# Rounding the attention weights on ScalarE and giving each of the first four attention steps three half projections

## The chip, the core and the metric

The kernel runs on one core of a Trainium2 chip. The time is that of the device for one launch, in microseconds (us): the median of three runs. One further run was taken with the hardware profiler; every row shown comes from that one.

## What is computed

One layer of a decoder: a mixer sublayer, a cross-attention to 256 memory tokens, and a SwiGLU feed-forward network, on 512 tokens of width 1024, in fp32. The change touches only the mixer, and in it only the causal stick-breaking attention (8 heads of 64) and the projections that run beside it:

```python
h = rms_norm(x, norm_mix[l])
proj = h @ w_in[l]
q_a, k_a, v_a, u_b, gate_b, gate_c, g_a, g_b = jnp.split(proj, split_points, axis=-1)
...
z = jnp.einsum('bhqd,bhkd->bhqk', qb, kb) * scale
log_fail = jnp.where(mask, jax.nn.log_sigmoid(-z), 0.0)
log_later = lax.cumsum(log_fail, axis=3, reverse=True) - log_fail
weights = jnp.where(mask, jnp.exp(jax.nn.log_sigmoid(z) + log_later), 0.0)
outs.append(jnp.einsum('bhqk,bhkd->bhqd', weights, vb))
```

## The kernel before

**Numbers in two parts.** TensorE is fed fp32r operands. To keep fp32 accuracy, every operand is split into a high part (the value rounded to fp32r, a copy) and a low part (value minus high part, a subtraction on VectorE), and each product is three matmuls: high by high, high by low, low by high (`mm3`, L154). For weights from memory the copy is on ScalarE (L150) and the subtraction on VectorE (L151).

**A projection** is one column block of 128 outputs: one load of 512 KB (L143, on SyncE's queue), the split, and 8 times three matmuls of 512 columns into one bank of `pmm`, a PSUM pool of two banks. It is done in two halves of 12 matmuls: `open_project` (L270) loads, splits and does the first half; `project` (L276) finishes it, and the caller (`qk_part`, `conv`, `gate`) reads the bank and frees it. Between the two halves the bank stays taken.

**An attention step** is one pair of heads `p` (0 to 3) with one block of 128 keys `kt`, taken from 3 down to 0; steps are numbered 0 to 15 in that order. It covers 128, 256, 384 or 512 queries of each of the two heads. For `kt` of 3 and 2 both heads share one tile of 256 or 512 columns, for 1 and 0 each has its own of 384 or 512.
- `scores` (L373): z on TensorE (L382 or L389); then `e` = softplus(z): Abs, Exp, Ln on ScalarE (L396 to L398), an add on VectorE (L399), the causal mask on GpSimd (`causal`, L355).
- `parts` (L408): adds the carry of the later key blocks (L420) and splits `e`: high part on ScalarE (L369), low part on VectorE (L370).
- `weights` (L428): TensorE adds the reverse cumulative sum into z's bank (L433, high part and then low part of each tile); the next carry (L438); `a` = Exp on ScalarE (L441); the mask on GpSimd (L355); then the high part `ah` (L449) and the low part `al` (L450), both on VectorE.
- `values` (L454): TensorE multiplies `ah` and `al` with the values (L461); after `kt` 0 the pair's output is copied, added and split (L469 to L472).

**The order of the work.** Within the loop over the steps (L519) TensorE's order is the program's: in step i it does its share of half projections, then `scores` of step i+1, `weights` of step i, `values` of step i-1. On the other engines a scheduler orders by its own estimate of when each instruction can start; `scores` and `parts` are raised in priority (100), the Exp of `weights` more so (150), the copies at L449 not. `fill_some` (L509) takes halves from a list of 22 column blocks, 44 halves in all: the next pair's q and k, then gate C, u and gate B of the convolution, pair after pair, and last four merge gates. After step i this many are done:

```python
FILL = ((3, 2, 3, 3), (2, 2, 3, 4))            # L33: first pair; each of the other three
shares = FILL[0] + (TT - 1) * FILL[1]          # L507
fill_some(n_fill * sum(shares[:i + 1]) / sum(shares))      # L524, rounded up by the loop of L510
```

At step 14 two small means are also taken through the same two banks of `pmm`: `var` at once after the share (L526), `varb` at the step's end (L538); `varb` is read by ScalarE (L121) and VectorE (L124). After the loop comes the merge, with sigmoids on ScalarE (L567) and one more gate.

Of the kernel before, what the change touches and what calls it, by code (L numbers as in the profile page):

```python
# [29 lines left out]
MEM_AT = (5, 7, 9, 11)  # L30
MEAN_AT = 14
EARLY = 2
FILL = ((3, 2, 3, 3), (2, 2, 3, 4))  # L33
WARM = 8
FIRST = 4

# [4 lines left out]
def hybrid_layer(ctx: ExitStack, tc: tile.TileContext, xT_d, memT_d, cols_d, wv_d, win_d,  # L41
                 wbr_d, wmix_d, wmq_d, wmk_d, wmv_d, wmo_d, wfi_d, wfo_d, out):
    nc = tc.nc
# [19 lines left out]
    def unit(s, cols=512):  # L63
        return upool.tile([P, cols], F32R, tag="u", name=nm(s), padded_shape=[P, 512])

    def tmp(s, cols=512):
        return tpool.tile([P, cols], F32, tag="t", name=nm(s), padded_shape=[P, 512])

    def f(ap):
        return ap.bitcast(F32)  # L70
# [273 lines left out]
    def span(kt):  # L344
        return kt * P, S - kt * P

    def by_head(t, kt):

        n = span(kt)[1]
        if 2 * n <= 512:  # L350
            return [t[0].rearrange("p (h n) -> p h n", n=n)]
        return [u[:, None, :] for u in t]

    def causal(t):
        nc.gpsimd.affine_select(out=t[:, :, :P], in_=t[:, :, :P], compare_op=ALU.is_gt, fill=0.0,  # L355
                                base=0, pattern=[[0, t.shape[1]], [1, P]], channel_multiplier=-1)
# [71 lines left out]
    def weights(p, kt):  # L428
        c0, n = span(kt)
        av[p, kt] = []  # L430
        for z, both in zip(zs[p, kt], sp[p, kt]):
            for part in both:
                nc.tensor.matmul(z, negtri, part, start=False, stop=True, skip_group_check=True)  # L433
        exp_a = []
        got = first.get((p, kt), [])
        with tc.high_priority(150):
            for r, z in zip(got, zs[p, kt]):
                nc.vector.tensor_tensor(out=r, in0=r, in1=z[0:1, :], op=ALU.subtract)  # L438
            for h, z in enumerate(zs[p, kt]):
                exp_a.append(tmp("a")[:, :z.shape[1]])  # L440
                exps.append(nc.scalar.activation(exp_a[h], z, AF.Exp))  # L441
            for h, r in enumerate(got):
                w = r.shape[1]
                nc.sync.dma_start(carries[kt % 2][P - 1:P, h * w:(h + 1) * w], r)
        for a in exp_a:
            causal(by_head([a], kt)[0])
            w = a.shape[1]
            ah, al = unit("ah")[:, :w], unit("al")[:, :w]
            nc.vector.tensor_copy(ah, a)  # L449
            nc.vector.tensor_tensor(out=al, in0=a, in1=f(ah), op=ALU.subtract)  # L450
            for i in range(w // n):
                av[p, kt].append((ah[:, i * n:(i + 1) * n], al[:, i * n:(i + 1) * n]))
# [53 lines left out]
    n_fill = len(fill)  # L506
    shares = FILL[0] + (TT - 1) * FILL[1]  # L507

# [9 lines left out]
    with tc.manual_schedule(engines={mybir.EngineType.PE}):  # L518
        for i in range(len(steps) + 1):  # L519
            if i in MEM_AT:  # L520
                mem_square(MEM_AT.index(i))
            if i == MEAN_AT - 2:
                mean = squares_mean(accm[:, 0, :], MT)
            fill_some(n_fill * sum(shares[:i + 1]) / sum(shares))  # L524
            if i == MEAN_AT:
                rm = mean[0]("rm", bank=mmtile)  # L526
            if i + 1 < len(steps):
                scores(*steps[i + 1])
            if i < len(steps):
                weights(*steps[i])  # L530
            else:
                gate(EARLY, 0)
            if i + 1 < len(steps):
                parts(*steps[i + 1])
            if i > 0:
                values(*steps[i - 1])
            if i == MEAN_AT:
                rmb = mean[1]("rmb", bank=mmtile)  # L538
# [555 lines left out]
```

## Time and profile before

| what | value |
|---|---|
| median of 3 runs | 860.76 us (860.56 to 861.03) |
| the profiled execution's own time | 860.98 us |
| its span, first to last instruction | 859.2 us |
| mean granted clock of TensorE | 0.999 |
| busy: PE, DVE, ACT, POOL | 850.5, 586.5, 431.1, 62.0 us |

In the rows, PE is TensorE's matmuls, PEld its weight loads, DVE is VectorE, ACT ScalarE, POOL GpSimd, SP SyncE. L12 is line 12 of the kernel. Matmuls are pipelined: a matmul of 512 columns shows as some 390 ns but the next starts after some 227 ns, so the distance of starts says how fast TensorE goes, and the busy column doesn't. A row of the timeline gives the start, the length of the merged rows, the engine, the line, the operation, output <- inputs, the count and, in brackets, the idle time before with what ended it.

### The profile page before, as it was taken

How to read it: one execution, taken by the hardware profiler on the slowest of the kernel's cores; microseconds unless marked ns; L12 is line 12 of the kernel's file. 1: busy time of each engine (PE TensorE's matmuls, PEld its weight loads, DVE VectorE, ACT ScalarE, POOL GpSimd, SP SyncE). 2: the span in 40 equal slices, each digit the busy share in tenths (PEclk: the TensorE clock that was granted, in tenths of full speed). 3: DMA queues.
4: the chain of work that ended last, by engine and by line, in shares of the span. 5: the costliest groups of instructions: out<-in, count | busy, mean ns of one | idle time of the engine just before them, and what ended most of it. 6: DMA issues, size and time to landing. Idle time of an engine off the chain costs nothing.

```text
span 859.2 us, 12693 instructions
## 1 busy us (share of the span) xinstructions
PE 850.5 (99%) x4912; PEld 748.6 (87%) x4912; DVE 586.5 (68%) x963; ACT 431.1 (50%) x750; POOL 62.0 (7%) x92
## 2 busy tenths in 40 slices
PE   9999999999999999999999999999999999999997
PEld 7877788888888898888888889999999999888897
DVE  8769898986454475555555779888887778533334
ACT  7566766665333344433444666555445556422335
POOL 1011111111000000000000101111111100000002
PEclk9999999999999999999999999999999999999999
DMA  8322331228333255422110527776777753322202
GB/s 295 132 90 77 120 111 62 74 99 266 111 103 111 96 177 184 143 98 98 50 67 33 137 54 202 187 182 172 185 188 195 182 147 127 119 98 99 73 1 98
DMA packets 42859, 108.34 MB, mean 126 GB/s; under 512 B 4656, under 2 KB 8752, under 8 KB 42800
## 3 DMA queue, kind: packets, MB, share of 16 engines
q1 hardware_dynamic: 36528, 95.72, 32.8%
q0 software_dynamic: 5984, 11.54, 8.2%
q8 instruction: 38, 0.62, 0.3%
q10 hardware_dynamic: 288, 0.29, 0.1%
q14 instruction: 21, 0.17, 0.1%
HBM read 104.36 MB, written 2.10 MB: 124 GB/s over the span
## 4 chain that ended last, share of the span: by engine, by line
PE 96%; DVE 2%; DMA 1%; issue 0%; POOL 0%; SPq 0%; DVEq 0%; ACT 0%; POOLq 0%
PE z L801 15%; PE y L801 7%; PE pr L155 7%; PE pr L156 7%; PE pr L157 7%; PE f L156 5%; PE f L157 5%; PE f L155 5%; PE v L801 4%; PE r L156 3%; PE r L155 3%; PE r L157 3%; PE v L261 3%; PE mq L156 2%; PE mq L157 2%; PE mq L155 2%
## 5 line engine op out<-in xcount | busy, mean ns | idle before, releaser
L150 ACT CAST wh<-wr 128x1024 fp32r<-128x1024 f32 x106 | 111.1, 1050 | 222.2 <-issue 98.6
L151 DVE TENSOR_TENSOR wl<-wr,wh 128x1024 fp32r<-128x1024 f32 x106 | 129.4, 1223 | 99.4 <-ACT wh L150 99.2
L155 PE MATMUL pr<-xgh,wh 128*128 128x512 f32 x288 | 112.6, 391 | 0.0
L156 PE MATMUL pr<-xgl,wh 128*128 128x512 f32 x288 | 112.4, 390 | 0.0
L157 PE MATMUL pr<-xgh,wl 128*128 128x512 f32 x288 | 112.3, 390 | 0.0
L156 PE MATMUL f<-actl,wh 128*128 128x512 f32 (+1 forms) x208 | 74.3, 357 | 0.0
L155 PE MATMUL f<-acth,wh 128*128 128x512 f32 (+1 forms) x208 | 74.2, 357 | 0.0
L157 PE MATMUL f<-acth,wl 128*128 128x512 f32 (+1 forms) x208 | 74.1, 357 | 0.0
L801 PE MATMUL z<-xdh,wf 128*128 128x256 f32 x352 | 70.4, 283 | 0.0
L157 PEld LDWEIGHTS pr<-xgh,wl 128*128 128x128 f32 x288 | 54.1, 188 | 11.3
L155 PEld LDWEIGHTS pr<-xgh,wh 128*128 128x128 f32 x288 | 54.1, 188 | 10.9
L156 PEld LDWEIGHTS pr<-xgl,wh 128*128 128x128 f32 x288 | 54.1, 188 | 10.8
L758 POOL DMA_DIRECT2D ws<-in_w_ffn_in_dram x22 | 26.6, 1208 | 469.0 <-DVE c L616 267.8
L801 PEld LDWEIGHTS z<-xdh,wf 128*128 128x128 f32 x352 | 58.0, 192 | 0.0
L821 ACT COPY sa<-z 128x256 f32<-128x256 f32 x44 | 16.4, 372 | 78.3 <-PE z L801 78.2
L801 PE MATMUL z<-xdl,wf 128*128 128x256 f32 x176 | 49.9, 283 | 0.0
L792 DVE TENSOR_TENSOR wf<-s,wf 128x512 fp32r<-128x512 f32 x44 | 30.3, 691 | 21.1 <-ACT wf L791 20.0
L155 PEld LDWEIGHTS f<-acth,wh 128*128 128x128 f32 x208 | 39.3, 189 | 5.8
L156 PEld LDWEIGHTS f<-actl,wh 128*128 128x128 f32 x208 | 39.3, 189 | 5.6
L157 PEld LDWEIGHTS f<-acth,wl 128*128 128x128 f32 x208 | 39.3, 189 | 5.5
L801 PE MATMUL v<-xoh,wf 128*128 128x256 f32 x176 | 35.5, 283 | 0.0
L801 PE MATMUL y<-xch,wf 128*128 128x256 f32 x176 | 35.5, 283 | 0.0
(281 smaller groups left out, 2134.8 us busy)
## 6 DMA issues: line engine op xcount, KB each, us to landing
wr<-in_w_in_dram SPq DMA_DIRECT2D x36, 512.0 KB, 3.3
ws<-in_w_ffn_in_dram SPq DMA_DIRECT2D x22, 512.0 KB, 3.8
wg<-in_w_ffn_in_dram SPq DMA_DIRECT2D x22, 512.0 KB, 4.2
ws<-in_w_ffn_in_dram POOLq DMA_DIRECT2D x22, 512.0 KB, 5.8
wr<-in_w_ffn_out_dram SPq DMA_DIRECT2D x22, 512.0 KB, 3.3
a<-in_w_ffn_in_dram SPq DMA_DIRECT2D x22, 256.0 KB, 4.5
wr<-in_w_branch_dram SPq DMA_DIRECT2D x8, 512.0 KB, 3.2
wr<-in_w_mem_k_dram SPq DMA_DIRECT2D x8, 512.0 KB, 3.2
```

Source lines behind the costliest of these rows:

```text
L150: after(nc.scalar.copy(h2, raw), lead[-1:])
L151: lows.append(nc.vector.tensor_tensor(out=l2, in0=raw, in1=f(h2), op=ALU.subtract))
L155: nc.tensor.matmul(ps, a[0], b[0], start=start, stop=False, **kw)
L156: nc.tensor.matmul(ps, a[0], b[1], start=False, stop=False, **kw)
L157: nc.tensor.matmul(ps, a[1], b[0], start=False, stop=stop, **kw)
L261: nc.tensor.matmul(vps[t], xg[k][a][:, sl], wv[k][b], start=k == 0 and (a, b) == (0, 0), stop=k == KD - 1 and a == 1)
L758: nc.gpsimd.dma_start(s13, a[:, 0:4:3, :], accum_op=ALU.add)
L792: nc.vector.tensor_tensor(out=lo, in0=raw, in1=f(hi), op=ALU.subtract)
L801: nc.tensor.matmul(ps[:, :HS], a, b, start=i < 3 and k == 0 and j == 0, stop=k == KP - 1 and j == 2, skip_group_check=True)
L821: nc.scalar.copy((s[:, :HS], None, None, s[:, HS:], t[:, :HS])[i], z)
```

## The change

Two edits. The copy that makes `ah` goes from VectorE to ScalarE, for all 24 tiles of attention weights. The shares of the first pair go from 3, 2, 3, 3 to 3, 3, 3, 3. The list still has 44 halves while the shares now add up to 45, and the loop rounds up, so the halves by step are

| step | 0 | 1 | 2 | 3 | 4 | 5 | 6 | 7 | 8 | 9 | 10 | 11 | 12 | 13 | 14 | 15 |
|---|---|---|---|---|---|---|---|---|---|---|---|---|---|---|---|---|
| before | 3 | 2 | 3 | 3 | 2 | 2 | 3 | 4 | 2 | 2 | 3 | 4 | 2 | 2 | 3 | 4 |
| after | 3 | 3 | 3 | 3 | 2 | 2 | 3 | 4 | 2 | 2 | 3 | 4 | 2 | 2 | 3 | 3 |

Step 1 gains one half and step 15 loses one; from step 1 to step 14 the list is one half further on, so that where a column block was finished and the next one opened, one is now opened and finished, and the other way round.

```diff
-FILL = ((3, 2, 3, 3), (2, 2, 3, 4))
+FILL = ((3, 3, 3, 3), (2, 2, 3, 4))
...
             ah, al = unit("ah")[:, :w], unit("al")[:, :w]
-            nc.vector.tensor_copy(ah, a)
+            nc.scalar.copy(ah, a)
             nc.vector.tensor_tensor(out=al, in0=a, in1=f(ah), op=ALU.subtract)
```

## Prediction

> **What bounds the kernel now.** I read the page's first part and its chain first, then the list of what TensorE waited for, then the attention stage by windows (the first pair of heads, and the last), then TensorE's timeline in that stage.
>
> ```profile
> span 859.2 us, 12693 instructions
> ...
> PE 850.5 (99%) x4912; PEld 748.6 (87%) x4912; DVE 586.5 (68%) x963; ACT 431.1 (50%) x750; POOL 62.0 (7%) x92
> ...
> PE 96%; DVE 2%; DMA 1%; issue 0%; POOL 0%; SPq 0%; DVEq 0%; ACT 0%; POOLq 0%
> ```
>
> ```profile
> PE z L433 <- DVE l L370: 0.9, 2, 0.5
> ```
>
> ```profile
> 28.70:77.00 48.30, 47.79 (x220) 38.43 (x221) 36.74 (x65) 28.94 (x57) 6.01 (x11) 1.00 0.28 94
> ...
> 155.00:193.00 38.00, 38.00 (x182) 31.23 (x181) 34.42 (x65) 24.34 (x48) 5.76 (x12) 1.00 0.24 84
> ```
>
> The chain is TensorE for 96% of the span. In the attention stage (20 to 210 us) TensorE is listed as waiting for one thing only: the low part `l` of step 1 and of step 3, 0.9 us in two waits. The windows (span, then busy PE, PEld, DVE, ACT, POOL) show why it is `l`: in the last pair's window VectorE is busy 34.42 of 38.00 us (91%), ScalarE 24.34 (64%). So no edit in this stage can win more than the time in which TensorE stands still, and the matmuls themselves are the same in number before and after. The timeline prices this, by starts:
>
> ```profile
> 49.54 0.39 PE L155 MATMUL pr<-xgh,wh 128*128 128x512 f32 x1
> ...
> 54.76 0.39 PE L157 MATMUL pr<-xgh,wl 128*128 128x512 f32 x1
> ...
> 55.79 0.49 PE L433 MATMUL z<-l,negtri 128*128 128x512 f32 x1
> 56.72 0.50 PE L433 MATMUL z<-l,negtri 128*128 128x512 f32 x1 [0.43 <-DVE l L370]
> 57.05 0.22 PE L461 MATMUL o<-ah,v 128*128 128x128 f32 x1
> ...
> 76.50 1.02 PE L433 MATMUL z<-l,negtri 128*128 128x512 f32 x3
> 77.99 0.50 PE L433 MATMUL z<-l,negtri 128*128 128x512 f32 x1 [0.47 <-DVE l L370]
> 78.33 0.33 PE L461 MATMUL o<-ah,v 128*128 128x384 f32 x1
> ```
>
> ```profile
> 92.64 0.73 PE L433 MATMUL z<-l,negtri 128*128 128x512 f32 x2
> 93.20 0.22 PE L461 MATMUL o<-ah,v 128*128 128x128 f32 x1
> ```
>
> ```profile
> 115.37 1.09 PE L433 MATMUL z<-l,negtri 128*128 128x512 f32 x4
> 116.30 0.33 PE L461 MATMUL o<-ah,v 128*128 128x384 f32 x1
> ```
>
> From the first two rows: 24 matmuls, so 23 distances in 5.22 us, 0.227 us each; **a half projection of 12 takes 2.72 us**. Step 1's `weights` took 57.05 - 55.79 = 1.26 us; the same step of the second pair, which didn't wait, 93.20 - 92.64 = 0.56: lost 0.70. Step 3's took 78.33 - 76.50 = 1.83 against 116.30 - 115.37 = 0.93: lost 0.90. **Together 1.60 us, 0.19% of the time, is all that the stage has to give by this reading.**
>
> **The change part by part.** *The third half in step 1.* It stands ahead of `weights` of step 1, so `l` has 2.72 us more; it was 0.43 us late by the idle time and 0.70 by starts. That wait goes whole: **-0.70**. Bounds: 0 (the whole wait reappears behind the added split and reading of a bank) and -0.70.
>
> *Step 3.* Its own share stays three, but the list is one half further on: u is finished one half sooner and gate B in the first half of step 3 instead of the second, so their VectorE work no longer stands among the instructions that make `l`. The two ahead of step 3's second `l` are now in part elsewhere:
>
> ```profile
> 75.44 0.69 DVE L334 TENSOR_TENSOR gb<-pr,r0b 128x512 f32<-128x512 f32 x1
> 76.05 0.68 DVE L370 TENSOR_TENSOR l<-e,l 128x512 fp32r<-128x512 f32 x1
> 76.65 0.69 DVE L335 TENSOR_TENSOR gb<-gb,cv 128x512 f32<-128x512 f32 x1
> 77.25 0.68 DVE L370 TENSOR_TENSOR l<-e,l 128x512 fp32r<-128x512 f32 x1
> ```
>
> The two `gb` rows put 0.60 + 0.60 us (by starts) before the second `l`, and the lateness was 0.47 idle. Taking them away alone suffices: **-0.90**, bounds 0 and -0.90.
>
> *The copies.* By the two sources of 24 tiles each (minimum, median, maximum in ns; L369 has the same shapes on ScalarE):
>
> ```profile
> L449 DVE CAST ah<-a x24: 294/419/625, 51.2 to 195.1; 128x512 fp32r<-128x512 f32 x12, 128x384 fp32r<-128x384 f32 x8, 128x256 fp32r<-128x256 f32 x4
> ```
>
> ```profile
> L369 ACT CAST l<-e x24: 406/560/622, 48.4 to 185.7; 128x512 fp32r<-128x512 f32 x12, 128x384 fp32r<-128x384 f32 x8, 128x256 fp32r<-128x256 f32 x4
> ```
>
> VectorE loses 24 x 0.419 = 10.1 us, ScalarE gets 24 x 0.560 = 13.4 us over some 145 us: for a pair 2.5 off 34.4 and 3.4 on 24.3, that is 84% and 73% of 38.0. Neither becomes the bound on average, and `values` reads `ah` a whole step later. What can hurt is the queue behind the copy on ScalarE: Abs, Exp and Ln of the next step, the weights' L150, and L369, which `weights` waits for. The tight places are the steps of 512 columns with two halves (5, 9, 13), where `l` lands just ahead of its matmul:
>
> ```profile
> 91.14 0.68 DVE L370 TENSOR_TENSOR l<-e,l 128x512 fp32r<-128x512 f32 x1
> ```
>
> ```profile
> 129.71 0.68 DVE L370 TENSOR_TENSOR l<-e,l 128x512 fp32r<-128x512 f32 x1
> ```
>
> ```profile
> 130.60 0.73 PE L433 MATMUL z<-l,negtri 128*128 128x512 f32 x2
> ```
>
> ```profile
> 167.89 0.68 DVE L370 TENSOR_TENSOR l<-e,l 128x512 fp32r<-128x512 f32 x1
> ```
>
> ```profile
> 168.57 0.73 PE L433 MATMUL z<-l,negtri 128*128 128x512 f32 x2
> ```
>
> The slack is 92.64 - 91.82 = 0.82, 130.60 - 130.39 = 0.21 and 168.57 - 168.57 = 0. In those steps the copy is that of 256 columns: 0.41 added on ScalarE, 0.29 gone on VectorE, 0.12 net if both stand in one chain. I take 0.1 at step 13 and 0.1 at step 9: **+0.2**, bounds -0 (no wait is there to be won) and the rival's 4.7 below.
>
> The Trainium skill (Perfetto Trace Analysis, Optimizing Scalar/DVE Operations) holds that an operation which either engine can do is faster on VectorE where a fast mode applies, and should go to ScalarE only where VectorE is saturated. The trace agrees with both halves of it here (0.419 against 0.560 us; VectorE at 91%). Its other table (ScalarE: Activation LUTs, Rules for kernel authors) sends plain arithmetic to VectorE without that condition; by that rule alone the move would be a loss, which is the slower rival below.
>
> *Step 15.* It loses a half, so `weights` of step 15 starts 2.72 us sooner. Rows of TensorE, ScalarE and VectorE there:
>
> ```profile
> 180.49 0.28 PE L197 MATMUL varb<-accl,mean_r 128*128 128x256 f32 x1
> ```
>
> ```profile
> 191.52 1.10 PE L433 MATMUL z<-l,negtri 128*128 128x512 f32 x4
> ```
>
> ```profile
> 182.64 0.47 ACT L121 ACTIVATE ry<-varb,eps_t 128x256 f32<-128x256 f32 x1
> ```
>
> ```profile
> 183.49 0.41 DVE L124 TENSOR_SCALAR rv<-varb 128x256 f32<-128x256 f32 x1
> ```
>
> ```profile
> 187.09 0.69 DVE L370 TENSOR_TENSOR l<-e,l 128x512 fp32r<-128x512 f32 x1
> ```
>
> `l` is whole at 187.78; the matmul at 191.52 - 2.72 = 188.80 still finds it, with 1.02 us left of 3.74. But the order of halves brings a **new wait**. Before, 40 halves were done after step 14 and no block was open; now 41 are, and one of the two banks is held by the open block while `varb` sits in the other. Step 15 finishes the open block (180.49 + 0.11 + 2.72 = 183.32) and must then open the next in `varb`'s bank, which is free when L124 has read it: 183.49 + 0.41 = 183.90. That is 0.58 us; if the two copies of step 14 (2 x 0.56) go ahead of L121 on ScalarE, its end becomes 182.64 + 1.12 + 0.47 = 184.23, 0.91 us. Behind this waiting matmul everything of TensorE is queued. **+0.7**, bounds 0 (the readers come sooner, now that VectorE has less to do) and 1.5 (the 0.91 and one more copy of 0.56 ahead of it). The same wait then covers the 2.72 us that `l` lost.
>
> *What moves along.* Each opened half issues a 512 KB load on SP's queue and, for u, a small fill on POOL; from step 1 on these come one half sooner, past the carries' transfers. TensorE is listed as waiting for no transfer, and the pace of loads stays one per two halves: I cost it at nothing. What hides it is the buffer of four blocks; were it gone, a load's landing time would show in each of the 22 openings.
>
> **Sum:** -0.70 - 0.90 + 0.2 + 0.7 = **-0.7 us**. The profiled execution took 860.98 us, span and 1.8 us around it; the sum is a difference against it. The median of the runs is 0.22 lower, and the forecast is 860.76 - 0.7 = **860.1 us**, in its own case 859.4 to 860.9.
>
> **The rivals.** *Both waits go and nothing comes* (the bank is read in time, the copies fit into ScalarE's gaps): -1.60, 859.2 us. For it: ScalarE is idle a third of the stage. Against: the bank's arithmetic above.
>
> *Nothing is won and the bank is paid*: the waits for `l` return in another step, as VectorE's reading of banks is shifted and not removed: +0.2 + 0.7, 861.7 us. For it: steps 9 and 13 have almost no slack. Against: 2.72 us is four times the wait at step 1.
>
> *ScalarE stands behind GpSimd* (slower). The copy needs the mask on `a`, and today VectorE already waits there:
>
> ```profile
> DVE ah L449 <- POOL a L355: 8.0, 10, 1.5
> ```
>
> That is 0.8 us a time and 1.5 at most. If the scheduler's order puts the copy ahead of L369 with that wait, ScalarE is held by it while `l`'s high part is queued behind. It decides from the point at which copy and wait exceed the slack of 0.82, 0.21 and 0. With 0.41 + 0.8 the three steps pay 0.39 + 1.00 + 1.21 = 2.6, with 0.41 + 1.5 they pay 1.09 + 1.70 + 1.91 = 4.7; with the other terms (-1.60 + 0.7) that is +1.7 to +3.8, 862.5 to 864.6, in the middle **863.5 us**. For it: ScalarE runs in order, and these steps are where VectorE's load is highest. Against: ahead of the copy ScalarE has the Ln of the next step to do (0.62 us), in which the mask runs. The chances weigh the ScalarE rule of the skill no higher than this.
>
> *The change doesn't do what it says* can only mean the shares: by the rounding they are three in each of the four steps, so this has no chance of its own.
>
> **How the numbers follow.** Forecast 0.50, both waits gone and nothing new 0.18, nothing won 0.14, slower 0.18. About 0.2%, 1.7 us, is what a measurement of this kernel can tell from no change: that is under 859.0 or over 862.5. Only the far end of the second case lies under it (0.06), and the whole of the last above it (0.18); 0.76 remains between. The range goes from 859.0 to 862.5, which leaves out 0.04 below and 0.16 above; what the bounds of single terms reach beyond it is in the slower rival.
>
> **What would show it.** Right: in the timeline after, L433 of steps 1 and 3 takes 0.56 and 0.93 us by starts; the list of TensorE's waits names the bank of `varb` (L121 or L124) at the opening in step 15, 0.6 to 0.9 us; VectorE's window falls to some 32 us of 38 and ScalarE's rises to 28. Wrong: waits of L433 at steps 5, 9 or 13 with ScalarE's L369 behind a copy, or a wait of `values` for `ah` at the stage's end, where the sigmoids' table load stands on ScalarE too.

## The result and the profile after

The changed kernel takes **865.40 us** (median of 6 runs, 862.84 to 865.95) against 860.99 us (6 runs, 860.56 to 861.13): ratio 1.0048, interval 1.0036 to 1.0059, 4.4 us slower. The forecast was 860.1 us with a range up to 862.5. The profiled execution took 865.49 us.

The page of the changed kernel, its span, its busy times (share, count) and its chain:

```profile
span 863.8 us, 12699 instructions
...
PE 853.1 (99%) x4912; PEld 750.3 (87%) x4912; DVE 580.0 (67%) x939; ACT 440.6 (51%) x774; POOL 60.9 (7%) x92
...
PE 98%; DVE 1%; ACT 0%; POOL 0%; issue 0%; DVEq 0%; POOLq 0%
```

What TensorE waited for in the attention stage (us in total, times, longest), the list that had the two waits for `l` before:

```profile
PE pr L155 <- DVE rv L124: 3.2, 1, 3.2
```

Both waits for `l` are gone and one new wait is there, at the place that the prediction named (the opening in step 15, for the reader of `varb`), at more than four times the length that it gave. TensorE's timeline of the changed kernel at steps 1, 3 and 15:

```profile
59.49 0.73 PE L433 MATMUL z<-l,negtri 128*128 128x512 f32 x2
60.05 0.22 PE L461 MATMUL o<-ah,v 128*128 128x128 f32 x1
...
79.50 1.09 PE L433 MATMUL z<-l,negtri 128*128 128x512 f32 x4
80.43 0.33 PE L461 MATMUL o<-ah,v 128*128 128x384 f32 x1
...
182.75 0.28 PE L197 MATMUL varb<-accl,mean_r 128*128 128x256 f32 x1
182.87 0.40 PE L155 MATMUL pr<-xgh,wh 128*128 128x512 f32 x1
...
185.39 0.39 PE L157 MATMUL pr<-xgh,wl 128*128 128x512 f32 x1
189.00 0.80 PE L155 MATMUL pr<-xgh,wh 128*128 128x512 f32 x1 [3.23 <-DVE rv L124]
189.60 0.63 PE L156 MATMUL pr<-xgl,wh 128*128 128x512 f32 x1
190.02 0.63 PE L157 MATMUL pr<-xgh,wl 128*128 128x512 f32 x1
...
192.08 0.40 PE L156 MATMUL pr<-xgl,wh 128*128 128x512 f32 x1
...
195.96 1.10 PE L433 MATMUL z<-l,negtri 128*128 128x512 f32 x4
```

By starts, steps 1 and 3 take 60.05 - 59.49 = 0.56 and 80.43 - 79.50 = 0.93 us: the 1.60 us were won whole. Step 15's three halves take 195.96 - 182.87 = 13.09 us where 36 matmuls at 0.227 are 8.17: **4.9 us lost**. Two parts make it up. From 185.39 to 189.00 are 3.61 us, 3.4 more than one distance. And after the wait the matmuls come 0.42 us apart (189.60 to 190.02) instead of 0.227, up to 192.08: 7 distances in 3.08 us instead of 1.59, 1.5 more. That is the clock; the windows (the third number from the right is the granted clock) show it in the same stretch of both kernels. Before:

```profile
180.00:200.00 20.00, 20.00 (x93) 16.72 (x92) 15.15 (x30) 12.90 (x22) 2.84 (x6) 1.00 0.47 149
```

After:

```profile
180.00:200.00 20.00, 16.77 (x76) 13.55 (x75) 12.18 (x23) 11.65 (x23) 2.97 (x6) 0.91 0.25 81
```

A clock of 0.91 over 20 us is, within its rounding, half speed for some 3.6 us; the trace's record of the granted clock has 0.50 from 188.55 to 191.96, 3.41 us. Of the 4.6 us between the two spans, +4.9 - 1.6 are thus told. Another 0.95 us lies ahead of the first projection, where both programs are the same: it starts at 28.66 us before and at 29.61 after. That piece is scatter of single executions and no effect of the change: a second profile of the changed kernel (`e14_after_again`, below) starts it at 28.76, and the sixteen profiles of this document at 28.35 to 29.61. The last 0.35 us lies in small pieces that were not followed.

Why L124 is late is to be read on VectorE. Before, from the first `e` of step 15 on:

```profile
182.06 0.68 DVE L399 SCALAR_TENSOR_TENSOR e<-z,e 128x512 f32<-128x512 f32 x1
182.66 0.55 DVE L450 TENSOR_TENSOR al<-a,ah 128x384 fp32r<-128x384 f32 x1
183.12 0.45 DVE L449 CAST ah<-a 128x384 fp32r<-128x384 f32 x1
183.49 0.41 DVE L124 TENSOR_SCALAR rv<-varb 128x256 f32<-128x256 f32 x1
183.82 0.67 DVE L399 SCALAR_TENSOR_TENSOR e<-z,e 128x512 f32<-128x512 f32 x1
```

After:

```profile
184.37 0.69 DVE L399 SCALAR_TENSOR_TENSOR e<-z,e 128x512 f32<-128x512 f32 x1 [1.36 <-ACT e L398]
185.09 0.56 DVE L420 TENSOR_TENSOR e<-e,carry 32x384 f32<-32x384 f32 x1
185.68 0.56 DVE L450 TENSOR_TENSOR al<-a,ah 128x384 fp32r<-128x384 f32 x1
186.15 0.69 DVE L399 SCALAR_TENSOR_TENSOR e<-z,e 128x512 f32<-128x512 f32 x1
186.75 0.68 DVE L370 TENSOR_TENSOR l<-e,l 128x512 fp32r<-128x512 f32 x1
187.47 0.55 DVE L420 TENSOR_TENSOR e<-e,carry 32x384 f32<-32x384 f32 x1
188.05 0.56 DVE L450 TENSOR_TENSOR al<-a,ah 128x384 fp32r<-128x384 f32 x1
188.53 0.42 DVE L124 TENSOR_SCALAR rv<-varb 128x256 f32<-128x256 f32 x1
```

The reader is the same 0.4 us, but the scheduler has put it behind the whole softplus of step 15 and both `al`: 188.53 - 182.75 = 5.8 us after `varb`, where it was 183.49 - 180.49 = 3.0. VectorE even stood idle for 1.36 us before the first of these rows, when `varb` had been written (182.75 + 0.28 = 183.03): it is not the amount of work on VectorE that kept L124 waiting.

### The profile page after: what moved, and what is told of

The parts are those of the page before. It is cut to its first block, busy times and chain, and to the rows that moved or that the text cites. A ratio compares the mean times of both kernels' runs of the same rounds, so it can differ in the third digit from the quotient of the medians.

```text
span 863.8 us, 12699 instructions
## 1 busy us (share of the span) xinstructions
PE 853.1 (99%) x4912; PEld 750.3 (87%) x4912; DVE 580.0 (67%) x939; ACT 440.6 (51%) x774; POOL 60.9 (7%) x92
## 4 chain that ended last, share of the span: by engine, by line
PE 98%; DVE 1%; ACT 0%; POOL 0%; issue 0%; DVEq 0%; POOLq 0%
PE z L801 15%; PE pr L155 8%; PE pr L156 7%; PE pr L157 7%; PE y L801 7%; PE f L156 5%; PE f L155 5%; PE f L157 5%; PE v L801 4%; PE r L156 3%; PE r L157 3%; PE r L155 3%; PE v L261 3%; PE mq L157 2%; PE mq L156 2%; PE mq L155 2%
```

## The experiments

The theory after the result, **bank**: the whole loss is one wait of TensorE for a bank of `pmm` held by one of the small means until its reader on VectorE or ScalarE has run, plus what that wait does to the clock; the copies and the shares are harmless where no projection can meet that bank. Rivals: **copies** (the work put on ScalarE costs by itself), **shares** (any shift of the list costs), and on the lateness of L124 a **buffer** theory (its output waits for a buffer that `al` frees) against an **order** theory (its place in the queue). Differences are against the kernel before in the same job: 861.26 us (23 runs) in the first, 861.10 (26) in the second, 861.18 (33) in the third, 861.36 (13) in the fourth.

### Each edit alone

Only the shares (`e1_shares_only`), that is the changed kernel with

```diff
-            nc.scalar.copy(ah, a)
+            nc.vector.tensor_copy(ah, a)
```

> Only the shares are changed; the copy for ah stays on VectorE. Bank theory (the loss is the wait for the bank of varb at step 15, long because al, which frees the buffer that L124 needs, waits for a copy in ScalarE's queue): the waits of steps 1 and 3 go (-1.6 us), the opening in step 15 waits only 0.6 to 1.5 us and TensorE's clock holds, so 860.0 to 861.0. Shares theory (the loss belongs to the shifted shares alone): the wait is 3 us or more as in the changed kernel, 863 to 866. Copies theory (the copies on ScalarE cost time by themselves): -1.6, 859.4.

Measured 864.49 us, +3.2, ratio 1.0037 (1.0025 to 1.0049). TensorE's wait:

```profile
PE pr L155 <- DVE rv L124: 2.9, 1, 2.9
```

The copies theory falls: without any copy on ScalarE the wait is there, nearly as long. So does my guess that `al` is late because of ScalarE's queue; here both `ah` and `al` are on VectorE, and L124 still comes behind both `al`. The bank theory's number (860.0 to 861.0) is missed too, and the time is where the shares theory had it; what tells these two apart are the runs below that keep the new shares and have no wait for the bank.

Only the copy (`e2_copy_only`):

```diff
-FILL = ((3, 3, 3, 3), (2, 2, 3, 4))
+FILL = ((3, 2, 3, 3), (2, 2, 3, 4))
```

> Only the copy goes to ScalarE; the shares stay 3, 2, 3, 3. Bank theory: no block is open at step 14, so no wait for a bank; the waits of steps 1 and 3 stay (0.9 us by the list) or shrink a little: 860.0 to 861.2. Shares theory: the same. Copies theory: the loss is here, 863 to 866, with waits of L433 or L461 for ScalarE.

Measured 861.92 us, +0.7, ratio 1.0006 (0.9997 to 1.0016): no difference that can be told, though above the 860.0 to 861.2 that was expected. Its waits in the stage add up to 1.5 us where the kernel before had 0.9:

```profile
PE pr L155 <- DVE rv L124: 0.8, 1, 0.8
PE pr L155 <- DVE gb L334: 0.5, 1, 0.5
PE z L433 <- DVE l L370: 0.2, 1, 0.2
```

The waits for `l` have shrunk from 0.9 to 0.2 us, so unloading VectorE does help there; but the bank of `varb` is waited for here too, though no block is open at step 14. My "no wait" was wrong: the second opening of step 15 can meet that bank with the old shares as well. Here L124 starts 186.75 - 180.72 = 6.0 us after `varb`, though the list was not shifted; before, the reader was simply in time.

### The means at another step, and another buffer

The changed kernel with the means one step earlier (`e3_mean_at_13`):

```diff
-MEAN_AT = 14
+MEAN_AT = 13
```

> The changed kernel with the two small means taken at step 13, where 38 halves are done and no block is open. Bank theory: the wait for varb's reader goes, TensorE's list has no wait of L155 for L124, the clock stays whole, and the gain of steps 1 and 3 is left: 859.1 to 860.0. Copies theory: the time stays at 863 to 866.

Measured 860.07 us, -1.2, ratio 0.9984 (0.9974 to 0.9993): faster than before. The list of TensorE's waits over the whole run has only its start:

```profile
PE warm L220 <- DVE neg L87: 1.6, 1, 1.6
PE v L261 <- DVE wvl L170: 0.3, 1, 0.3
```

The second mean's temporaries in the large pool (`e4_temps_elsewhere`):

```diff
         def new(t):
+            if s == "rmb":
+                return f(unit(t))[:, :n]
             return tmp(t, n) if n > TT else spool.tile([P, n], F32, tag=t, name=nm(t))
```

> The changed kernel with the three temporaries of varb's chain taken from the large pool of 50 buffers instead of the pool of seven. Buffer theory: L124 no longer waits for the second al, it starts about when L121 does or before it; the wait of the opening in step 15 falls from 3.2 to 0.5 to 2 us and the clock holds: 859.8 to 861.5. Queue theory (L124 is late only by its place behind other work on VectorE and ScalarE): the wait stays at 3 us and the time at 863 to 866.

Measured 864.79 us, +3.5, ratio 1.0038 (1.0026 to 1.0049); the line numbers are two higher here:

```profile
PE pr L157 <- DVE rv L126: 3.2, 1, 3.2
```

The buffer theory falls: with buffers to spare the wait is the same 3.2 us. This kernel's profiled execution happened to keep its clock (mean 0.999) and took 863.13 us. Of the six runs two kept it, at 862.76 and 863.13 us; the four with 0.997 or less took 864.33 to 865.94.

### The order of the reader, and the half taken elsewhere

The second mean raised in priority (`e5_prio`):

```diff
-                rmb = mean[1]("rmb", bank=mmtile)
+                with tc.high_priority(200):
+                    rmb = mean[1]("rmb", bank=mmtile)
```

> The changed kernel with the second mean (varb's matmuls and their readers L121 and L124) raised in priority above the softplus of step 15. Order theory (L124 is late because VectorE's order has the whole softplus of step 15 ahead of it): L124 moves ahead of the second e, the wait of the opening in step 15 falls from 3.2 to 0.3 to 1.5 us, 1.5 to 4 us less than the changed kernel: -1.5 to +0.5 against before. Readiness theory (the scheduler believes varb to be ready late, so a priority moves nothing): the wait stays near 3 us and the time 3 to 4 us over before.

Measured 862.82 us, +1.7, ratio 1.0021 (1.0012 to 1.0030). The wait and the reader's place on VectorE:

```profile
PE pr L155 <- DVE rv L124: 1.8, 1, 1.8
```

```profile
185.23 0.68 DVE L399 SCALAR_TENSOR_TENSOR e<-z,e 128x512 f32<-128x512 f32 x1
185.83 0.41 DVE L124 TENSOR_SCALAR rv<-varb 128x256 f32<-128x256 f32 x1
```

L124 now stands behind the second `e` instead of behind the second `al`, and the wait falls from 3.2 to 1.8 us. Order, then, but not as far as the expectation had it: L124 does not get ahead of that `e`, so the gain is 1.4 us of wait where 1.7 or more was expected, and the time of +1.7 lies outside the -1.5 to +0.5 of the order theory. Why the scheduler does not start it sooner is its own estimate, which no run here shows.

The half taken from step 14 instead of 15 (`e6_half_from_14`), and the same with the copy on VectorE (`e7_half_from_14_dve`):

```diff
-    shares = FILL[0] + (TT - 1) * FILL[1]
+    shares = FILL[0] + 2 * FILL[1] + (2, 2, 2, 4)
```

> The changed kernel with the extra half of step 1 taken from step 14 (shares of the last pair 2, 2, 2, 4, so the shares add up to 44), with the means still at step 14. Bank theory: 40 halves are done after step 14, no block is open, and the wait for varb's bank is at most that of the copy alone (0.8 us): -1.6 to -0.6 us against before. Shares theory (any shift of the list costs): 3 to 4 us over before.

> As the run before it, but the copy for ah stays on VectorE. Bank theory, with the copies as good on either engine: the same within 0.5 us, -1.6 to -0.6 against before. If the copies on ScalarE cost by themselves (0.7 us, as the run with the copy alone hints): 0.3 to 0.8 us faster than that kernel. If they help by unloading VectorE: slower than it, with a wait of L433 for l left.

Measured 861.50 us (+0.4, ratio 1.0005, 0.9996 to 1.0015) and 861.51 us (+0.4, 1.0005, 0.9995 to 1.0015). First the wait of the one, then of the other:

```profile
PE pr L155 <- DVE rv L124: 1.5, 1, 1.5
```

```profile
PE pr L155 <- DVE rv L124: 1.9, 1, 1.9
```

A miss: no block is open after step 14 and the wait is still 1.5 to 1.9 us, which eats the 1.6 won. With an open block the first opening of step 15 meets the bank, some 2.8 us after `varb`; without one the second does, some 5.7 us after it. The two medians differ by 0.01 us, which is chance at this closeness: the intervals reach 0.9 us either way, and the waits differ by 0.4.

The means at step 13 with the copy on VectorE (`e8_mean_at_13_dve`), that is `e3_mean_at_13` with the diff of `e1_shares_only`:

> Shares changed and the means at step 13, with the copy for ah on VectorE. Bank theory: no wait for varb's bank, -1.6 to -0.9 against before. Against the same kernel with the copy on ScalarE (1.2 us under before): if the copy is worth nothing, the same within 0.4 us; if VectorE's relief is needed at steps 5, 9 and 13, slower by up to 1 us with waits of L433 for l.

Measured 864.17 us, +3.1, ratio 1.0032 (1.0017 to 1.0048):

```profile
PE pr L155 <- ACT rv L126: 2.7, 1, 2.7
```

A second miss, and the best lesson: shares and step of the means are those of the kernel that was 1.2 us faster than before, and moving 24 copies to another engine puts the reader of the *first* mean (L126, `var`) 2.7 us late. Whether the bank is free in time hangs on where the scheduler's order happens to put one short instruction.

### The bank taken away, in all four combinations

If the bank is the whole loss, the two edits must show their own worth once no projection can meet it. At step 15 no further `scores` come, so the z pool has free banks:

```diff
-MEAN_AT = 14
+MEAN_AT = 15
...
-                rm = mean[0]("rm", bank=mmtile)
+                rm = mean[0]("rm", bank=ztile)
...
-                rmb = mean[1]("rmb", bank=mmtile)
+                rmb = mean[1]("rmb", bank=ztile)
```

Both edits:

> Both edits, with the two means at step 15 in banks of the z pool, which no later step uses, so no projection can wait for their readers. Bank theory: TensorE's list has no wait of L155 for L121, L124 or L126, and the gain of steps 1 and 3 is left whole: -1.3 to -1.7 us against before, at any clock. Rival (the shifted shares themselves cost, the bank is only where it shows): the wait reappears elsewhere, +1 or more.

Only the shares:

> Only the shares, with the means out of the way as in the run before it. Bank theory: no wait for a bank. If the shares alone bring the gain of steps 1 and 3: -1.3 to -1.7 and no difference to the run with both edits beyond 0.3 us. If the gain of step 3 came from unloading VectorE: a wait of L433 of 0.5 us or more there, -0.4 to -0.9.

Neither:

> Neither edit, the means out of the way: what moving the means is worth by itself. Bank theory: before had no wait for a bank, so the waits of steps 1 and 3 stay and the time is that of before within 0.3 us.

Only the copy:

> Only the copy, the means out of the way. With the copy alone the bank wait was 0.8 us, a wait behind a gate's reader 0.5, one for l 0.2, and the time 0.7 over before. Bank theory: the 0.8 goes and the rest stays: -0.4 to +0.2 against before. If ScalarE's queue costs by itself: +0.5 or more, with waits for L369 or L449.

| means in banks of their own | copy on VectorE | copy on ScalarE |
|---|---|---|
| shares 3, 2, 3, 3 | 860.98 us, -0.2, ratio 0.9998 (0.9989 to 1.0006) | 860.74 us, -0.4, 0.9996 (0.9987 to 1.0005) |
| shares 3, 3, 3, 3 | 859.68 us, -1.5, 0.9984 (0.9975 to 0.9993) | 859.79 us, -1.4, 0.9985 (0.9976 to 0.9994) |

TensorE's list for the stage has one entry with neither edit and none in the other three:

```profile
PE z L433 <- DVE l L370: 0.7, 2, 0.5
```

Three came as the bank theory had it. With the copy alone the 0.8 us of the bank went as it had it, but the two waits that were to stay (0.5 and 0.2) are gone from the list too, so with the means out of the way either edit by itself removes the listed waits for `l`. By the medians the shares are worth 1.3 us with the copy on VectorE, 0.95 on ScalarE; the copy 0.24 without the new shares and nothing (0.11 the other way) with them, both within the intervals. The profiles give the copy alone more: from the start of the first projection to the first L433 of step 15 it is 161.61 us with the copy alone, 162.49 with neither edit, 161.12 with the shares and 161.22 with both. How much the copy is worth by itself is therefore open, between 0.2 and 0.9 us. The two lower kernels beat the kernel before, and the copy is not needed for it.

### The clock

The changed kernel with TensorE kept at work during the wait (`e13_keep_busy`; the twelve matmuls' results are not used):

```diff
+            if i == len(steps) - 1:
+                fill_some(42)
+                busy = ztile("busy")
+                for _ in range(12):
+                    nc.tensor.matmul(busy, neg1, neg1[:, None, :].broadcast_to([P, S // P, P]),
+                                     start=True, stop=True)
```

> The changed kernel with 12 idle matmuls of 512 columns (results not used) put on TensorE in step 15 between the finished block and the next opening, into a free bank of the z pool: they fill 2.7 us of the wait for varb's reader and add no work after it. Clock theory (a wait of 3 us or more lets the clock fall to half for one stretch of 3.4 us, 1.7 us lost): the wait shown falls to about 0.5, the clock never falls there, all runs lie near the fastest of the changed kernel, 1.6 to 2.2 us over before, and the spread closes. Rival (the slow runs of the changed kernel have another cause, or the idle matmuls only delay): the median stays 3 to 5 us over before.

> The changed kernel once more, beside the run before it. Clock theory: two groups of runs, those with a mean clock of 0.998 and more 1.6 to 2.2 us over before, those below 3.3 us and more over it. Rival: times that don't go with the clock.

Measured 863.74 us (7 runs, 862.88 to 864.02), +2.4, ratio 1.0025 (1.0014 to 1.0036), beside 865.33 us (6 runs, 862.84 to 866.41), +4.0, 1.0042 (1.0030 to 1.0054), for the changed kernel again. TensorE's timeline with the filling:

```profile
185.39 2.91 PE L528 MATMUL busy<-neg 128*128 128x512 f32 x12
188.77 0.50 PE L155 MATMUL pr<-xgh,wh 128*128 128x512 f32 x1 [0.48 <-DVE rv L124]
```

and the window of the changed kernel's second profile:

```profile
180.00:200.00 20.00, 16.77 (x69) 13.34 (x66) 11.67 (x22) 10.91 (x22) 2.97 (x6) 0.83 0.21 70
```

The bank comes free at about the same time (188.77 against 189.00), no work is taken away, and the median falls by 1.6 us, with mean clocks of 0.998 and 0.999 in all seven runs. Without the filling the six runs have 0.995, 0.999, 0.995, 0.997, 0.998 and 0.996 at 865.98, 862.84, 866.41, 865.30, 863.67 and 865.36 us: the higher the clock, the shorter the run. The two with a clock of 0.998 and more are 1.5 and 2.3 us over before, the other four 3.9 to 5.1. In the second profile the half speed lasted two stretches, 0.83 over 20 us or 6.8 us. The clock theory holds; the 2.4 us over before is a little more than the 2.2 expected, and close to what the unfilled kernel takes when its clock does not fall.

## Why the prediction was wrong

- *What bounds the kernel*: right. 1.60 us was all that the stage had to give: the best kernels gave 1.4 and 1.5.
- *The third half in step 1, and step 3*: right, -0.70 and -0.90 by the timeline. The two waits also shrink by the copy alone (0.9 to 0.2 us on the list, to nothing with the means in banks of their own), which the prediction did not count: the two edits in part win the same time.
- *The copies, +0.2 at steps 9 and 13*: in the changed kernel no wait of L433 came at any step; the four combinations put the copy at -0.24 and +0.11. That VectorE was busy for 91% of a window, and is the faster engine for this copy (0.419 against 0.560 us), did not settle whether moving it pays. The sizes were right: by the source in the changed kernel the copy takes 0.566 us on ScalarE (median of the 24), and a pair's window has VectorE at 32.24 and ScalarE at 28.49 of 38.00 us:

```profile
81.20:119.20 38.00, 38.00 (x179) 30.72 (x178) 32.24 (x52) 28.49 (x56) 5.46 (x13) 1.00 0.32 105
```

- *The slower rival* (ScalarE behind GpSimd): it did not happen. In the changed kernel ScalarE waited 1.3 us for the mask in three waits, 0.5 at most:

```profile
ACT ah L449 <- POOL a L355: 1.3, 3, 0.5
```

  The time came out slower for another reason, so that rival's 863.5 is not borne out.
- *Step 15, +0.7 with bounds 0 and 1.5*: **this is the step that failed.** The wait was named, with its instruction and its reason, and measured 4.9 us: 3.4 of standing still and some 1.5 of half clock. Two mistakes. The first: L124's start was taken from the trace of before, 3.0 us after `varb`, with two copies added on ScalarE. But the order on VectorE and ScalarE is no part of the program here; a scheduler makes it anew from the whole list, and after the shift it put L124 behind the softplus: 5.8 us. The bound should have been the end of what could be put ahead of it, the last `l` of the step. In the trace of before that ends at 187.78; with L124 behind it the bank is free at 187.78 + 0.41 = 188.19, and the wait's bound would have been 188.19 - 183.32 = 4.9 us of standing still, which holds the 3.4. The second: a wait of TensorE was priced at its length, and the clock was not in the sum. With 4.9 for this term and nothing for the copies the sum is -1.6 + 4.9 = +3.3 us; the profiles' 4.6 are this, the 0.95 of scatter at the start and the 0.35 not followed. Why the scheduler chose that place stays open.
- *"The open block brings the wait"*: half right. It brings the meeting one half of a projection sooner, but the runs with the half taken from step 14, and the one with the copy alone, met the bank without it.
- *What moves along* (the loads), costed at nothing: right, TensorE's list names no transfer.

## What to carry to other kernels

Where a scheduler orders an engine, the place of a small instruction in the trace of before says nothing on its place after an edit elsewhere; whoever frees a buffer that the bound engine will want next has to be bounded by all that may be put ahead of it, or given a buffer of its own. A short wait on a full TensorE must be priced with the clock that it may cost. When an edit loses, taking the one shared resource away and trying all combinations of the edits tells in four runs which of them were good.

## What the runs showed of the hardware

The clock fell after waits of less than 3.4 us, and not every time. Runs with a mean clock of 0.997 or less, which the kernel before never had (0.998 to 1.000 in the 95 runs of the four jobs), by the longest wait that the kernel's profile shows:

| longest wait in the stage, us | kernel | such runs |
|---|---|---|
| 3.2 | changed kernel, both times | 9 of 12 |
| 3.2 | e4_temps_elsewhere | 4 of 6 |
| 2.9 | e1_shares_only | 5 of 6 |
| 2.7 | e8_mean_at_13_dve | 3 of 5 |
| 1.9 | e7_half_from_14_dve | 1 of 10 |
| 1.8 | e5_prio | 5 of 10 |
| 1.5 | e6_half_from_14 | 0 of 10 |
| 0.8 | e2_copy_only | 0 of 10 |
| 0.5 | e13_keep_busy | 0 of 7 |

The Trainium skill (TensorE: Matmul & The Clock Gate, Why this matters for your kernels) asks for no gap over some 3 us between bursts of matmuls, and its Part 1 gives an idle window of about 3.4 us that runs freely. The half speed seen here came in stretches of one or two such lengths (3.41 us in the changed kernel, 6.83 in its second profile), and its chance nature fits a window that starts at no fixed moment. The limit of 3 us does not fit: the clock fell in half of the runs of a kernel whose profile shows a wait of 1.8 us, and the profile of `e7_half_from_14_dve` has a wait of 1.9 us with half speed right behind it, from 188.49 to 191.90 us.

The traces' record of the granted clock shows what the chance consists of. In all sixteen profiles the clock, once up, changes only after whole multiples of 3.413 us (in the changed kernel after 53, then after 1, then after 196). If each run is cut into pieces of this length from the moment at which the clock went up, the most that TensorE stood still within one piece is 2.78, 2.55, 2.17 and 1.87 us in the four profiles in which the clock fell at that piece's end (the changed kernel, `e1_shares_only`, `e14_after_again`, `e7_half_from_14_dve`), and 1.91, 1.69, 1.48 and 1.42 in those with a wait of 1.5 us or more in which it didn't (`e4_temps_elsewhere`, `e5_prio`, `e6_half_from_14`, `e8_mean_at_13_dve`). So the same wait of 3.2 us cost the clock where 2.78 or 2.17 of it fell into one piece, and did not where the cut left 1.91 and 1.32. By these eight profiles the border is at some 1.9 us of 3.41; the ends of matmuls in a trace are modelled, so the second digit is not to be trusted.
